# Token gather and expert combination as fp32r products, with the small loads on ScalarE's queue

## The chip, the cores and the metric

The kernel runs on one core of a Trainium2 chip. The metric is the device time of one execution in microseconds (us), median of several runs. In the text TensorE, VectorE, ScalarE, GpSimd and SyncE stand for the rows PE, DVE, ACT, POOL and SP.

## The reference

Two transformer blocks with conditioning, and a second model block behind them, on one sequence of 256 tokens of width 1024. There are three mixers, and behind each stands a mixture of 32 experts, of which every token uses two. Cut to the expert layer:

```python
def _hier_moe(h, w_group, b_group, w_expert, b_expert, w1, w3, w2):
    g_sel = argmax(h @ w_group + b_group)             # one of 4 groups
    top_v, top_i = top_k(expert logits of the group, 2)
    gate = p_g * softmax(top_v)
    ...
    xr = xt[tok]                                      # tokens of expert e
    y = (silu(xr @ w1[e]) * (xr @ w3[e])) @ w2[e]     # 1024 -> 512 -> 1024
    return segment_sum(y * w_row, token)              # weighted sum back to the tokens
```

All data are fp32; the weights of one expert layer are 32 x 3 x 1024 x 512 x 4 bytes, 201 MB.

## The kernel before

The program runs even mixer, expert stage 0, odd mixer, expert stage 1, mixer of the second block, expert stage 2, final norm. Weights stream through a ring of 18 slots in SBUF, 1 MB each (8 KB per partition). `Net.pump` takes a free slot and issues one DMA on SyncE's queue for the next weight piece in a planned order; `done` gives a slot back when the product that read it is emitted, and pumps again; `release` gives back slots held for other things; `reserve` keeps some free slots from the stream for later use. In stage 2 a few further slots ("more") are at hand. So the stream runs ahead by at most the ring, and when the ring is full it stops until a product gives a slot back.

An expert stage (`moe`) has 16 pairs of experts. Before the pairs `route` finds each token's experts and its rank within an expert (`mk` the mask, a triangular product for the ranks, `rk` the rank, `wt` the weight), and `overflow` holds a branch for experts with more than CAP = 64 tokens, which is not taken here. Pair p then does, in TensorE's order:

- `up(p, "g")`, `up(p, "u")`: the two up products, with 4 slots each. `sg` is the silu of the first; `hh` is the product of both.
- `gather(p+1)`: the token matrix `h` (256 tokens x 1024, normalised, in one ring slot) times a one-hot `u` (token to place), fp32, 128 columns; VectorE and ScalarE write the result to `xg` with scale and shift (`affine`).
- `gather_w(p+1)`: transposes the weighted one-hot `uw` to `pg`.
- `turn(p)`: transposes `hh` to `ht`. `down(p)`: the down product with 4 slots, evicted to `y` with the gate factor `ga`.
- `combine(p, t)`: `pg` times `y`, fp32, added by VectorE to token tile t of `x`. For pair p-1 it runs between the products of pair p.

The last pair uses `down_last`, which makes the down product and the addition in four pieces. At pair 0, behind the first up product, `start` emits work for the next stage, and with it small loads: the attention bias (`bias_load`) and router weights (`router`) in stage 0, router weights and constants of the second block (`second_setup`) in stage 1. They are issued on GpSimd's queue, which has nothing else to do there and runs ahead.

A fp32 matmul appears as two records in the trace, an fp32r one as one.

## Time and profile before

| | |
|---|---|
| runs | 2140.69, 2144.75, 2133.42 us; median 2140.69 |
| profiled execution | span 2133.2 us; no time of its own is given beside the span |
| TensorE busy | 2020.9 us, 95% of the span |
| VectorE, ScalarE, GpSimd busy | 793.1, 405.3, 256.1 us |
| DMA | 725.46 MB, 340 GB/s on the mean, 400 to 404 GB/s in most slices of the expert stages |

Busy time is a mean over stages with different limits: the mixers lie near slices 1 to 4, 14 to 17 and 26 to 31 of 40, where the DMA rate is low, and the expert stages between and behind them. The span of the profiled execution stands 7.5 us below the median of the runs and 0.2 below the lowest.

### The profile page before, as it was taken

The numbers are of one execution on the slowest core, as the hardware profiler recorded it, in microseconds if no ns is written. First come the engines' busy times: TensorE is split into PE (matmuls) and PEld (weight loads), VectorE is DVE, ScalarE is ACT, GpSimd is POOL, SyncE is SP. The second block draws the span as 40 slices with busy tenths as digits, with TensorE's granted clock in tenths as the row PEclk, the third lists the DMA queues.
The fourth block names the chain that finished last, engine by engine and source line by source line (L and its number), as shares of the span: only waits on it lengthen the run. The fifth ranks groups of instructions, "written<-read, shape, count | busy, mean of one in ns | idle before, by whom it ended". The sixth has DMA issues, their size and how long they took to land. (4 is left out here: it accounts for less than half of the span.)

```text
span 2133.2 us, 26516 instructions
## 1 busy us (share of the span) xinstructions
PE 2020.9 (95%) x10698; PEld 1077.0 (50%) x10698; DVE 793.1 (37%) x1576; ACT 405.3 (19%) x836; POOL 256.1 (12%) x202
## 2 busy tenths in 40 slices
PE   6889899999999998899999999998899999999997
PEld 3646444434443767543444434686887443444443
DVE  3665222222222667322222222467666122222222
ACT  1423100100000343200000000254543100100101
POOL 1422000000000343200000000143433000000000
PEclk8998999999999999999999999999999999999999
DMA  9797999999999866999999999922457999999997
GB/s 318 245 321 297 366 400 402 403 400 401 404 400 390 311 226 237 336 403 400 400 404 400 400 403 402 310 93 66 133 217 257 381 403 401 400 402 403 400 401 267
DMA packets 279205, 725.46 MB, mean 340 GB/s; under 512 B 18267, under 2 KB 33587, under 8 KB 279069
## 3 DMA queue, kind: packets, MB, share of 16 engines
q1 hardware_dynamic: 269776, 716.84, 88.9%
q0 software_dynamic: 1456, 3.59, 0.6%
q10 hardware_dynamic: 7836, 3.17, 0.6%
q8 instruction: 91, 1.49, 0.3%
q14 instruction: 46, 0.37, 0.0%
HBM read 722.48 MB, written 1.07 MB: 339 GB/s over the span
## 5 line engine op out<-in xcount | busy, mean ns | idle before, releaser
L256 PE MATMUL ps<-slot,xg 128*64 128x512 f32 x2952 | 666.4, 601 | 20.0 <-PEq L1712 12.1
L256 PEld LDWEIGHTS ps<-slot,xg 128*64 128x64 f32 x2952 | 209.3, 138 | 458.6 <-issue 419.6
L256 PE MATMUL ps<-slot 128*128 128x256 f32 (+8 forms) x2230 | 370.4, 327 | 13.9 <-DVE slot L457 9.5
L256 PE MATMUL ps<-slot,ht 128*64 128x512 f32 (+1 forms) x1592 | 343.3, 572 | 6.4 <-DVE ht L249 3.5
L256 PEld LDWEIGHTS ps<-slot 128*128 128x128 f32 (+3 forms) x2230 | 301.4, 187 | 73.2 <-issue 12.9
L1860 DVE TENSOR_TENSOR x<-x,ps 128x512 f32<-128x512 f32 x180 | 120.8, 684 | 322.0 <-PE ps L256 321.2
L256 PEld LDWEIGHTS ps<-slot,ht 128*64 128x64 f32 x1592 | 113.9, 138 | 222.5 <-issue 181.0
L458 POOL TENSOR_TENSOR slot<-slot 128x512 fp32r<-128x512 f32 (+2 forms) x108 | 165.0, 1545 | 263.9 <-ACT slot L456 242.5
L256 PEld LDWEIGHTS ps<-u,slot 128*128 128x128 f32 x1536 | 175.1, 192 | 37.2 <-issue 36.5
L256 PE MATMUL ps<-y,pg 128*128 128x512 f32 (+1 forms) x408 | 187.0, 582 | 0.0
L256 PE MATMUL ps<-u,slot 128*128 128x128 f32 x1536 | 184.2, 278 | 0.0
L1825 DVE TENSOR_TENSOR hh<-sg,ps 128x512 f32<-128x512 f32 x48 | 50.6, 1054 | 340.6 <-PE ps L256 325.6
L1821 ACT ACTIVATE sg<-ps 128x512 f32<-128x512 f32 x48 | 28.7, 597 | 606.4 <-PE ps L256 606.4
L457 DVE TENSOR_TENSOR slot<-slot 128x512 fp32r<-128x512 f32 (+2 forms) x108 | 110.4, 1036 | 53.1 <-ACT slot L456 52.8
L374 POOL TENSOR_TENSOR xr<-xr,mhalf 128x2 f32<-128x2 f32 x7 | 5.0, 711 | 1022.1 <-DVE xr L373 1004.7
L456 ACT CAST slot<-slot 128x1024 fp32r<-128x1024 f32 (+2 forms) x108 | 106.6, 1020 | 46.3 <-PE ps L256 27.3
L256 PEld LDWEIGHTS ps<-y,pg 128*128 128x128 f32 x408 | 69.5, 190 | 86.3 <-issue 84.7
L394 ACT ACTIVATE xg<-ps,cf 128x128 f32<-128x128 f32 x128 | 48.5, 457 | 317.5 <-PE ps L256 317.5
L1850 DVE TENSOR_TENSOR y<-ps,ga 128x512 f32<-128x512 f32 x60 | 41.5, 692 | 171.3 <-PE ps L256 171.3
L398 DVE TENSOR_SCALAR xg<-ps,cf 128x128 f32<-128x128 f32 x128 | 43.9, 404 | 81.0 <-PE ps L256 80.8
L1889 POOL TENSOR_TENSOR slot<-x,rows 128x512 f32<-128x512 f32 x2 | 2.6, 1276 | 480.2 <-DVE x L1885 480.2
L256 PE MATMUL ps<-slot,condz 128*32 128x512 f32 x384 | 48.0, 620 | 6.6 <-DMA slot<-ada_w 6.6
(349 smaller groups left out, 1337.8 us busy)
## 6 DMA issues: line engine op xcount, KB each, us to landing
slot<-moe_w SPq DMA_DIRECT2D x376, 1024.0 KB, 16.8
slot<-w_gate SPq DMA_DIRECT2D x57, 1024.0 KB, 16.2
slot<-w_up SPq DMA_DIRECT2D x56, 1024.0 KB, 20.5
slot<-w_down SPq DMA_DIRECT2D x55, 1024.0 KB, 21.0
slot<-ada_w SPq DMA_DIRECT2D x48, 1024.0 KB, 8.8
slot<-w_in SPq DMA_DIRECT2D x20, 1024.0 KB, 4.8
slot<-odd_w_in SPq DMA_DIRECT2D x12, 1024.0 KB, 13.4
slot<-even_w_in SPq DMA_DIRECT2D x9, 1024.0 KB, 16.9
```

What stands on the lines that cost most here:

```text
L256: self.nc.tensor.matmul(out, lhsT=lhsT, rhs=rhs, start=start, stop=stop)
L374: self.nc.gpsimd.tensor_tensor(out, out, self.mhalf[:, :cols], op=OP.pow)
L394: self.nc.scalar.activation(out, p, AF.Identity, scale=a, bias=nb[:, k:k + 1])
L398: self.nc.vector.tensor_scalar(out, p, a, nb[:, k:k + 1], op0=OP.mult, op1=OP.add)
L456: nc.scalar.copy(wh, src)
L457: nc.vector.tensor_sub(wl[:, 0], src[:, 0], wh[:, 0].bitcast(FT))
L458: nc.gpsimd.tensor_sub(wl[:, 1], src[:, 1], wh[:, 1].bitcast(FT))
L1821: nc.scalar.activation(sg, ps, AF.Silu)
L1825: nc.vector.tensor_mul(hh.rearrange("s k p -> s p k"), st["sg", p].rearrange("s (p k) -> s p k", k=4), ps.rearrange("s (p k) -> s p k", k=4))
L1850: nc.vector.tensor_mul(y[:, sl], ps, self.ga[:, sl])
L1860: nc.vector.tensor_add(self.x[:, t, sl], self.x[:, t, sl], ps)
L1889: (nc.gpsimd, nc.vector)[n % 2].tensor_mul(fo[:, :, sl], xs, fw[:, None, sl].to_broadcast([P, NT, T]))
```

## The change

The gather and the combination become fp32r products. The token matrix is kept as a rounded part `hh` and a remainder `hl`, in two ring slots instead of one; `u` is 0 or 1 for four experts at once, and each gather serves two pairs with 256 columns. The transposed weighted one-hot becomes a 0/1 mask `pg`, and a sum over it, `ws`, one weight for each place, that is multiplied into `hh` of the experts (renamed `ha`). The down product is split into `yh` and `yl` by `parts`, and a combination adds the products of both. All DMAs of GpSimd's queue go to ScalarE's. The mixers end with `reserve=2`, and the slots of the token matrix are released at pair 13.

```diff
     def bias_load(self, i, raw):
         v = self.bvec
-        self.nc.gpsimd.dma_start(raw, bass.AP(tensor=v.tensor, offset=v.offset + i * 8 * 384,
+        self.nc.scalar.dma_start(raw, bass.AP(tensor=v.tensor, offset=v.offset + i * 8 * 384,
...
-        self.release(5, reserve=1)
+        self.release(5, reserve=2)
...
             self.S[nm] = g.tile(shape, FT, name=nm)
-            nc.gpsimd.dma_start(self.S[nm], src)
+            nc.scalar.dma_start(self.S[nm], src)
...
-        nc.gpsimd.dma_start(br[:, 0:4], bg.to_broadcast([P, 4]))
-        nc.gpsimd.dma_start(br[:, 4:36], be.to_broadcast([P, 32]))
...
+        nc.scalar.dma_start(br[:, 0:4], bg.to_broadcast([P, 4]))
+        nc.scalar.dma_start(br[:, 4:36], be.to_broadcast([P, 32]))
...
         nc.vector.tensor_mul(v4(mk), gb, r4(ob))
+        rest()
         p = self.psum((P, NT, E))
...
-            h = self.slot().rearrange("p (t k q) -> p t k q", t=NT, k=KC)
+            hh, hl = (self.slot(FR).rearrange("p (t k q) -> p t k q", t=NT, k=KC) for i in range(2))
             r = self.x_rstd()
             self.route_turn(1)
             self.route_logits(1)
             xv = self.x.rearrange("q t (p k) -> q t k p", k=KC)
-            nc.scalar.activation(h[:, 0], xv[:, 0], AF.Copy, scale=r[:, 0:1])
-            nc.gpsimd.tensor_scalar(h[:, 1], xv[:, 1], r[:, 1:2], None, op0=OP.mult)
-            rk, wt, ti, finish, late = self.route(g, r, mods)
+            for t in range(NT):
+                nc.scalar.activation(hh[:, t], xv[:, t], AF.Copy, scale=r[:, t:t + 1])
+            h0 = g.tile([P, KC, 2 * P], FT, name="xg").rearrange("p (t k) q -> p t (k q)", t=NT)[:, 0]
+            h0 = h0.rearrange("p (k q) -> p k q", k=KC)
+            nc.gpsimd.tensor_scalar(h0, xv[:, 0], r[:, 0:1], None, op0=OP.mult)
+            nc.gpsimd.tensor_sub(hl[:, 0], h0, hh[:, 0].bitcast(FT))
+
+            def rest():
+                nc.vector.scalar_tensor_tensor(hl[:, 1], xv[:, 1], r[:, 1:2], hh[:, 1].bitcast(FT),
+                                               op0=OP.mult, op1=OP.subtract)
+
+            rk, wt, ti, finish, late = self.route(g, r, mods, rest)
             NP = E // 2
             st = {}
             if l == 2:
                 fw = self.rows[1]
-            bc = lambda a, p: a[:, :, 2 * p:2 * p + 2, None].to_broadcast([P, NT, 2, CAP])
-
-            def onehot(p):
-                u = g.tile([P, NT, 2, CAP], FT, name="u", bufs=2)
-                nc.vector.tensor_tensor(u, self.iota[:, None, None, :].to_broadcast([P, NT, 2, CAP]), bc(rk, p),
+            bc = lambda a, e, n: a[:, :, e:e + n, None].to_broadcast([P, NT, n, CAP])
+
+            def onehot(j):
+                u = g.tile([P, NT, 4, CAP], FR, name="u", bufs=2)
+                nc.vector.tensor_tensor(u, self.iota[:, None, None, :].to_broadcast([P, NT, 4, CAP]), bc(rk, 4 * j, 4),
                                         op=OP.is_equal)
-                st["u", p] = u
+                st["u", j] = u
 
             def weighted(p):
-                uw = g.tile([P, NT, 2, CAP], FT, name="uw", bufs=2)
-                nc.vector.tensor_mul(uw, st["u", p], bc(wt, p))
+                uw = g.tile([P, NT, 2, CAP], FT, name="uw")
+                u = st["u", p // 2][:, :, p % 2 * 2:p % 2 * 2 + 2].bitcast(FT)
+                nc.vector.tensor_mul(uw, u, bc(wt, 2 * p, 2))
                 st["uw", p] = uw
 
-            def gather(p):
-                xg = g.tile([P, KC, P], FT, name="xg")
-                m = 4 if p else 2
-                for k0 in range(0, KC, m):
-                    ps = self.psum((P, P * m))
-                    for k in range(m):
+            def gather(j):
+                xg = g.tile([P, KC, 2 * P], FT, name="xg")
+                u = st["u", j].rearrange("p t a s -> p t (a s)")
+                for k0 in range(0, KC, 2):
+                    ps = self.psum().rearrange("p (k s) -> p k s", k=2)
+                    for k in range(2):
                         for t in range(NT):
-                            self.mm(ps[:, P * k:P * k + P], h[:, t, k0 + k], st["u", p][:, t], t == 0, t == NT - 1)
-                    for k in range(m):
-                        self.affine(xg[:, k0 + k], ps[:, P * k:P * k + P], k0 + k, "av"[k0 // m % 2])
-                st["xg", p] = xg
+                            for i, part in enumerate((hh, hl)):
+                                self.mm(ps[:, k], part[:, t, k0 + k], u[:, t], t + i == 0, t + i == 2)
+                    for k in range(2):
+                        self.affine(xg[:, k0 + k], ps[:, k], k0 + k, "av"[k])
+                st["xg"] = xg
 
             def gather_w(p):
                 ps = self.psum((P, T))
                 for t in range(NT):
                     self.tr(ps[:, P * t:P * t + P], st["uw", p][:, t].rearrange("p a s -> p (a s)"))
-                pg = g.tile([P, T], FT, name="pg", bufs=2)
-                self.copy(pg, ps, "a")
-                st["pg", p] = pg
+                pg = g.tile([P, T], FR, name="pg", bufs=2)
+                nc.vector.tensor_scalar(pg, ps, 0.0, None, op0=OP.is_gt)
+                ws = g.tile([P, 1], FT, name="ws", bufs=2)
+                nc.vector.tensor_reduce(ws, ps, axis=AX.X, op=OP.add)
+                st["pg", p], st["ws", p] = pg, ws
...
-                        self.mm(ps[64 * s:64 * s + 64], st["xg", p][:, k, 64 * s:64 * s + 64],
+                        self.mm(ps[64 * s:64 * s + 64], st["xg"][:, k, p % 2 * P + 64 * s:p % 2 * P + 64 * s + 64],
...
-                    hh = g.tile([P, 512], FT, name="hh").rearrange("p (k s) -> p k s", k=4)
-                    nc.vector.tensor_mul(hh.rearrange("s k p -> s p k"),
-                                         st["sg", p].rearrange("s (p k) -> s p k", k=4),
-                                         ps.rearrange("s (p k) -> s p k", k=4))
-                    st["hh", p] = hh
+                    ha = g.tile([P, 512], FT, name="hh").rearrange("p (k s) -> p k s", k=4)
+                    nc.vector.scalar_tensor_tensor(ha.rearrange("s k p -> s p k"),
+                                                   st["sg", p].rearrange("s (p k) -> s p k", k=4), st["ws", p],
+                                                   ps.rearrange("s (p k) -> s p k", k=4), op0=OP.mult, op1=OP.mult)
...
+            def parts(p, sl, ps):
+                if sl.start == 0:
+                    st["y", p] = [g.tile([P, D], FR, name=nm) for nm in ("yh", "yl")]
+                yh, yl = (y[:, sl] for y in st["y", p])
+                if gate:
+                    y = g.tile([P, 512], FT, name="sg", bufs=2)[:, :sl.stop - sl.start]
+                    nc.vector.tensor_mul(y, ps, self.ga[:, sl])
+                    nc.scalar.copy(yh, y)
+                    nc.gpsimd.tensor_sub(yl, y, yh.bitcast(FT))
+                else:
+                    nc.scalar.copy(yh, ps)
+                    nc.vector.tensor_sub(yl, ps, yh.bitcast(FT))
...
             def combine(p, t):
                 for n in range(2):
                     ps = self.psum()
                     sl = slice(512 * n, 512 * n + 512)
-                    self.mm(ps, st["pg", p][:, P * t:P * t + P], st["y", p][:, sl], True, True)
+                    for i, y in enumerate(st["y", p]):
+                        self.mm(ps, st["pg", p][:, P * t:P * t + P], y[:, sl], i == 0, i == 1)
                     nc.vector.tensor_add(self.x[:, t, sl], self.x[:, t, sl], ps)
...
             weighted(0)
             for p in range(NP):
                 last = p == NP - 1
                 if last:
-                    self.reserve += slots
+                    self.reserve += max(0, slots - 2)
                     if l == 2:
                         fo = self.slot().rearrange("p (t d) -> p t d", t=NT)
                 else:
-                    onehot(p + 1)
+                    if p % 2:
+                        onehot(p // 2 + 1)
                     weighted(p + 1)
                 if last:
                     up(p, "g", lambda: combine(p - 1, 0))
                     up(p, "u", lambda: combine(p - 1, 1))
-                    self.release()
                     turn(p)
                 else:
                     up(p, "g")
                             nc.scalar.dma_start(fw, self.A["final_norm_2"].rearrange("(o n) -> o n", o=1)
                                                 .to_broadcast([P, D]))
                     up(p, "u")
-                    gather(p + 1)
+                    if p % 2:
+                        gather(p // 2 + 1)
+                        if p == NP - 3:
+                            self.release(2, reserve=min(2, slots))
```

SyncE issues the weight loads. Here is its order around stage 0's branch (L1711 to L1726; `moe_w` are expert weights), before:

```order
L192 DMA slot<-moe_w 128x2x1024 x8
L192 DMA slot<-moe_w 128x4x512 x4
L192 DMA slot<-moe_w 128x2x1024 x4
L1711 TENSOR_LOAD ti
L1712 COMPARE_AND_BRANCH
```

and after the change:

```order
L193 DMA slot<-moe_w 128x2x1024 x8
L193 DMA slot<-moe_w 128x4x512 x4
L193 DMA slot<-moe_w 128x2x1024 x3
L1713 TENSOR_LOAD ti
L1714 COMPARE_AND_BRANCH
```

One weight load has moved from ahead of the branch to behind it: 15 instead of 16.

VectorE's order in `route` between the mask and the one-hot, before:

```order
L1662 TENSOR_TENSOR mk<-ohg,ob 128x64
L1669 SCALAR_TENSOR_TENSOR rk<-ps,mk 128x64
L1670 TENSOR_SCALAR rk<-rk 128x64
L1779 TENSOR_TENSOR u<-km,rk 128x256
L1678 TENSOR_REDUCE top<-rk 128x1
```

and after the change:

```order
L1663 TENSOR_TENSOR mk<-ohg,ob 128x64
L1779 SCALAR_TENSOR_TENSOR slot<-x,xr,slot 128x1024
L1671 SCALAR_TENSOR_TENSOR rk<-ps,mk 128x64
L1672 TENSOR_SCALAR rk<-rk 128x64
L1791 TENSOR_TENSOR u<-km,rk 128x512
L1680 TENSOR_REDUCE top<-rk 128x1
```

The remainder of token tile 1 (`rest`) has come in between mask and rank, and `u` is twice as wide.

ScalarE's order at the first pair of stage 0, before (`sg` is the silu of the first up product):

```order
L1821 ACTIVATE sg<-ps 128x512
L247 COPY pg<-ps 128x256
L247 COPY ga<-ps 128x512 x2
L394 ACTIVATE xg<-ps,cf 128x128 x4
L247 COPY pg<-ps 128x256
L1821 ACTIVATE sg<-ps 128x512
```

and after the change:

```order
L1837 ACTIVATE sg<-ps 128x512
L579 DMA bias_1470<-bvec 128x8x256
L248 COPY ga<-ps 128x512 x2
L1589 DMA wr<-moe_w_group 128x8x4
L1590 DMA wr<-moe_w_expert 128x8x32
L1591 DMA br<-moe_b_group 128x4
L1592 DMA br<-moe_b_expert 128x32
L1861 CAST yh<-sg 128x512 x2
L1837 ACTIVATE sg<-ps 128x512
```

The bias and router loads stand behind the silu, the copies of `pg` are gone from ScalarE, and the gather's evictions of pair 0 are gone with the gather, which now follows at pair 1.

## Rows read from the trace of the kernel before

**Rows 1.** The page: span, busy time per engine, DMA share and rate in 40 slices.
```profile
span 2133.2 us, 26516 instructions
...
PE 2020.9 (95%) x10698; PEld 1077.0 (50%) x10698; DVE 793.1 (37%) x1576; ACT 405.3 (19%) x836; POOL 256.1 (12%) x202
...
DMA  9797999999999866999999999922457999999997
GB/s 318 245 321 297 366 400 402 403 400 401 404 400 390 311 226 237 336 403 400 400 404 400 400 403 402 310 93 66 133 217 257 381 403 401 400 402 403 400 401 267
```

**Rows 2.** Busy time in five stretches: four stage starts, one middle; columns in the first row.
```profile
core 0: us, PE busy (x) PEld busy (x) DVE busy (x) ACT busy (x) POOL busy (x), PEclk, DMA share, GB/s
226.00:236.00 10.00, 9.60 (x36) 3.51 (x37) 0.00 (x0) 0.84 (x2) 0.00 (x0) 0.83 0.95 298
252.00:256.00 4.00, 4.00 (x22) 1.56 (x19) 0.69 (x1) 0.00 (x0) 0.00 (x0) 1.00 0.67 207
880.00:890.00 10.00, 9.63 (x35) 3.36 (x36) 0.00 (x0) 0.18 (x1) 3.77 (x7) 0.75 0.85 228
1646.00:1656.00 10.00, 7.46 (x48) 4.80 (x48) 5.12 (x24) 2.84 (x7) 0.00 (x0) 1.00 0.33 111
1100.00:1150.00 50.00, 50.00 (x256) 21.94 (x252) 14.08 (x26) 4.36 (x11) 0.00 (x0) 1.00 1.03 403
```

**Rows 3.** The page's DMA issues: the weight slots, KB each, us to landing.
```profile
slot<-moe_w SPq DMA_DIRECT2D x376, 1024.0 KB, 16.8
```

**Rows 4.** Timeline of TensorE, 576 to 612: start, us, tiles, shapes, count.
```profile
578.99 7.04 PE L256 MATMUL ps<-slot,xg 128*64 128x512 f32 x32
...
594.89 3.84 PE L256 MATMUL ps<-u,slot 128*128 128x128 f32 x32
...
599.22 1.88 PE L256 MATMUL ps<-y,pg 128*128 128x512 f32 x4
...
607.95 4.46 PE L256 MATMUL ps<-slot,xg 128*64 128x512 f32 x20
```

**Rows 5.** Timeline of TensorE, 640 to 707, the end of the first expert stage.
```profile
652.47 1.94 PE L256 MATMUL ps<-slot,xg 128*64 128x512 f32 x8 [0.62 <-DMA slot<-moe_w]
...
660.48 7.09 PE L256 MATMUL ps<-slot,ht 128*64 128x512 f32 x32
```

**Rows 6.** Timeline of TensorE, 1170 to 1362, the end of the second.
```profile
1310.14 1.94 PE L256 MATMUL ps<-slot,xg 128*64 128x512 f32 x8 [0.62 <-DMA slot<-moe_w]
```

**Rows 7.** Timeline of TensorE, 1985 to 2134, the end of the third.
```profile
2100.30 1.94 PE L256 MATMUL ps<-more,xg 128*64 128x512 f32 x8 [0.63 <-DMA more<-w_up]
```

**Rows 8.** Timeline of TensorE: fp32r products of other stages, 24 matmuls each.
```profile
1519.67 3.04 PE L256 MATMUL ps<-slot,wx 128*128 128x256 f32 x24
...
195.98 5.74 PE L256 MATMUL ps<-slot 128*128 128x512 f32 x24
```

**Rows 9.** Groups of instructions by line and shape: busy, mean ns, idle before.
```profile
L1378 DVE TENSOR_TENSOR slot<-slot 128x1024 f32<-128x1024 f32 x1 | 1.2, 1225 | 1.1 <-ACT slot L1377 1.1
...
L1768 ACT ACTIVATE slot<-x,xr 128x1024 f32<-128x1024 f32 x3 | 6.6, 2186 | 1.3 <-POOL xr L374 1.3
...
L458 POOL TENSOR_TENSOR slot<-slot 128x256 fp32r<-128x256 f32 x4 | 3.7, 935 | 10.2 <-ACT slot L456 10.2
...
L1875 DVE TENSOR_TENSOR y<-ps,ga 128x256 f32<-128x256 f32 x8 | 3.4, 425 | 11.5 <-PE ps L256 11.5
```

**Rows 10.** Timeline of VectorE, 204 to 262, behind the rank product.
```profile
216.08 0.23 DVE L1669 SCALAR_TENSOR_TENSOR rk<-ps,mk 128x64 f32<-128x64 f32 x1 [1.01 <-PE ps L256]
...
216.57 0.42 DVE L1779 TENSOR_TENSOR u<-km,rk 128x256 f32<-128x256 f32 x1
```

**Rows 11.** DMA queue of GpSimd, 215 to 240, then 878 to 895: packets, MB, share.
```profile
q0 software_dynamic: 416, 1.21, 15.0%
...
q0 software_dynamic: 624, 1.16, 29.8%
```

**Rows 12.** Timeline of GpSimd, 219 to 224: its DMA issues.
```profile
219.71 0.98 POOL L578 DMA_DIRECT2D bias<-bvec  x1 [6.90 <-DVE wt L1697]
```

More of the change, by code (lines that the diff above doesn't have):

```diff
@@ L30 @@
 SLOT = 2048
+SCRATCH = 2048
 EVEN = (1, 1, 4, 1, 1, 2, 2)
@@ L1565, in second @@
             self.weave(self.nsa_prep(g), self.nsa_attn(g, sc), self.hgrn(g, q8), stream())
-        self.release(6, reserve=1)
+        self.release(6, reserve=2)
     def plan_moe(self, l):
@@ L1722, in overflow @@
                     for k in range(4):
-                        self.tr(p[:, k], h[:, t, k0 + k])
+                        for i, part in enumerate(h):
+                            self.mm(p[:, k], part[:, t, k0 + k].bitcast(FT), self.ident, i == 0, i == 1)
                     for k in range(4):
@@ L1728, in overflow @@
                 nc.scalar.dma_start(wc, wd[bass.ds(e, 1)].rearrange("e p t -> (e p) t"))
-                ho = g.tile([P, 4, T], FT, name="y")
+                ho = g.tile([P, 4, T], FT, name="ho", tag="yh")
                 chunk = lambda tag: g.tile([P, 512], FT, name=tag)
@@ L1836, in turn @@
                 st["ht", p] = ht
+            def parts(p, sl, ps):
[10 more added lines that the diff above has]
+                    nc.vector.tensor_sub(yl, ps, yh.bitcast(FT))
             def down(p):
-                y = g.tile([P, D], FT, name="y")
                 for n in range(2):
@@ L1848, in down @@
                     self.done((l, "d", p, 2 * n), (l, "d", p, 2 * n + 1))
-                    if gate:
-                        nc.vector.tensor_mul(y[:, sl], ps, self.ga[:, sl])
-                    else:
-                        self.copy(y[:, sl], ps, "av"[n])
-                st["y", p] = y
+                    parts(p, sl, ps)
             def combine(p, t):
@@ L1873, in piece @@
                     self.done((l, "d", p, n))
-                    if gate:
-                        nc.vector.tensor_mul(y[:, sl], ps, self.ga[:, sl])
-                    else:
-                        self.copy(y[:, sl], ps, "a")
+                    parts(p, sl, ps)
                 def add(n):
@@ L1882, in add @@
                     for t in range(NT):
-                        self.mm(ps[:, t], st["pg", p][:, P * t:P * t + P], y[:, sl], True, True)
+                        for i, y in enumerate(st["y", p]):
+                            self.mm(ps[:, t], st["pg", p][:, P * t:P * t + P], y[:, sl], i == 0, i == 1)
                     xs = self.x[:, :, sl]
```

16 lines of the change are left out of this document (8 added, 8 removed).

## The prediction

> **What bounds the kernel now.** I read the page first. TensorE is busy for most of the span, which would make it the bound, but the slices say otherwise: through most of the three expert stages the DMA row stands at 9 and the rate lies flat near 400 GB/s [rows 1]. The fifth window of [rows 2] puts numbers on it: 50 us in the middle of the second stage, DMA share 1.03, 403 GB/s. One weight slot is 1024 KB [rows 3], that is 1,048,576 B / 403 GB/s = 2.60 us, and a pair of experts has 12 slots, so the stream needs 31.2 us per pair. TensorE's timeline gives its own need: from 578.99 to 607.95 one pair takes 28.96 us [rows 4]. TensorE is therefore the faster of the two; it starts each stage behind a full ring and catches up with the stream. In the first stage it meets it only at pair 14: the wait of 0.62 us before 652.47 ends on a landing [rows 5]; in the second such waits repeat up to 1310.14 [rows 6], in the third up to 2100.30 [rows 7]. After the last of them TensorE works off what is left. The length of a stage is thus the time when its last-waited slot lands plus TensorE's work behind that. I call this landing W.
>
> Where does the stream lose time? Only where the ring is full and nothing is given back: at the start of each stage. The first four windows of [rows 2] give it against 403: 226 to 236 loses 10 x (1 - 298/403) = 2.6 us, 252 to 256 (TensorE gathers and turns, and gives back no slot) 4 x (1 - 207/403) = 1.9, 880 to 890 4.3, 1646 to 1656 7.2. Everything that moves W is decided there.
>
> **TensorE's work in a pair.** The gather of a pair, 32 records, takes 3.84 us, a combination of one token tile 1.88 [rows 4]. An fp32r matmul of 256 columns takes 3.04/24 = 0.127 us and one of 512 columns 5.74/24 = 0.239 [rows 8]. The new gather has 32 matmuls of 256 columns for two pairs: 4.05 us instead of 7.68. The new combination has 4 of 512 columns per tile: 0.96 instead of 1.88. So TensorE saves (7.68 - 4.05)/2 + 2 x 0.92 = 3.7 us per pair at most; in odd pairs eight evictions of 256 columns stand on VectorE ahead of the copy to ht, at 0.425 us or more each [rows 9], 3.4 us where TensorE has 1.0 of combination to do; averaged over both pairs that gives about 1.2 to 1.4 back, and TensorE's pair is near 26.7 us. Over 48 pairs that is more than 100 us, and I count none of it: the stream needs 31.2, TensorE will only wait more. It counts behind W alone.
>
> **Gains behind W.** In the first stage W is 652.47 and the second half of pair 14's down product starts at about 660.48 + 3.5 = 664.0, W + 11.5 [rows 5]. Its last slot lands four slots behind W, at W + 10.4, so of the shorter gather only about 1.0 counts. Then two combinations, 0.92 each: 1.9. In the last pair four add products halve (about 0.5 each, 2.0), but the eviction before each becomes three steps: VectorE 0.425 and a ScalarE cast, then a GpSimd subtraction, where 256 columns took 0.935 [rows 9]; about 1.5 of the 2.0 is given back. Together 3.4 us, and as much in the second stage. In the third the last waits lie inside the last pair [rows 7], and only 0.4 (one combination, against the next landing) and 1.4 of the tail remain: 1.8. Gains: 8.6 us.
>
> **Losses before W.** (a) *A slot less.* The token matrix now takes two ring slots. SP's order shows 15 weight loads ahead of the branch where there were 16, in all three stages one less. The ring is full at the start, so each stage loads one slot later: 3 x 2.6 = 7.8. The bounds are 0 (if the ring had not filled) and 7.8; the idle windows of [rows 2] put it at the upper end. The Trainium skill (DMA: Bandwidth & Descriptors, section Specifications) gives about 358 GB/s as a core's share of HBM. By it a slot would take 2.93 us and this term be 8.8. The trace moves 403 and the sum goes by that.
>
> (b) *The first product starts later.* VectorE now computes a 128x1024 remainder between mk and rk, and the one-hot u doubles (0.42 to about 0.8). A plain 128x1024 VectorE operation on contiguous data takes 1225 ns; a ScalarE pass over the same strided reading takes 2186 [rows 9]. So 1.2 to 2.4 us, of which 1.01 lies in the wait for the rank product that stands there anyway [rows 10]. With u: 0.6 to 1.8 later; I take 1.2, as a single-input stride is what slowed the ScalarE pass, and here one of two inputs is strided. Gather, first product and first give-back all follow: 3 x 1.2 = 3.6.
>
> (c) *The small loads.* Before, GpSimd's queue moved the bias and the router weights of the first stage while the ring was full, 1.21 MB at 15.0% of 25 us = 3.75 us of all engines; in the second stage 1.16 MB, 29.8% of 17 us = 5.07 [rows 11]. They ran in those idle windows, free. Now ScalarE issues them behind its first silu, when slots are coming back and the weight stream has work: each us that they take moves W. By bytes at 403 they need 3.0 and 2.9; by the queue's records 3.75 and 5.07. I take 3.7 (1 MB in one large piece, so what was recorded) and 3.6 (small pieces can overlap with others'). Sum 7.3, bounds 5.9 and 8.8, or 0 if they still find idle time.
>
> (d) *Shared lanes.* ScalarE's DMAs wait, like SP's, for the DMA eight places earlier in the common sequence; GpSimd's had lanes of their own. In the second stage 15 loads stand between weight loads. I take 1.0 (0 to 6).
>
> (e) *One stall goes.* Pair 0 no longer gathers, so the give-back pause at 252 to 256 shrinks from 6 us to under 3: -2.0 (0 to -2.0).
>
> (f) The first mixer's ScalarE issues five DMAs that GpSimd issued: 0.5. The longest GpSimd issue took 0.98 us [rows 12], so 0 to 4.9.
>
> VectorE and ScalarE work that is added inside the pairs (mask, sum of weights, cast, remainder) lies beside 12 weight slots per pair; VectorE was 37% busy [rows 1]. If that cover went, the ht copy would be the first to be late, and it delays TensorE, not the stream.
>
> **Sum.** 7.8 + 3.6 + 7.3 + 1.0 - 2.0 + 0.5 = 18.2 lost, 8.6 gained: +9.6 us on the profiled span of 2133.2. That span equals the lowest of the three runs and lies 7.5 below their median of 2140.69; their mean is 2139.6. Against the mean: 2149.
>
> **Rivals.** *The stream gets faster (ends faster than before).* If the weight stream's pace depends on how soon TensorE gives slots back, a quicker TensorE speeds it up. 576 slots at 2.565 us instead of 2.60 save 20 us: 2129; from 408 GB/s on it decides. Against it: the share of 1.03 in [rows 2] leaves the engines no free time, and the rate is as flat where TensorE waits as where it lags [rows 1]. The Trainium skill (DMA: Bandwidth & Descriptors, section Latency and other measured facts) guesses that GpSimd's descriptor rings slow two of the DMA engines; without its DMAs the stream might then gain. No row here shows such an effect: the flat stretches ran without that queue. Chance 0.12.
>
> *The start costs are hidden.* If the small loads land before the stream has work and the ring's lost slot is refilled within the same idle spell, (a) to (d) vanish, and -8.6 - 2.0 stays: about 2130. For it: the third stage idles 7.2 us [rows 2], more than a slot. Against it: idle time there is the ring being full, which a smaller ring lengthens. Chance 0.15.
>
> *Shared lanes block SP (slower).* A weight load queued behind a ScalarE load that itself waits idles the stream; with (c), (b) at the upper ends (+1.5, +1.8) and (d) at 6: +18 or more, 2158 to 2165. It decides once SP pauses over 2 us after the first give-back. Chance 0.18.
>
> **How the numbers follow.** The forecast, 2142 to 2157, has 0.55. 0.5% is 10.7 us, about what a measurement can tell from no change; so faster is under 2130.0, slower over 2151.4. The forecast gives 0.38 same and 0.17 slower; the faster stream 0.12 faster; hidden costs 0.06 faster and 0.09 same; lanes 0.18 slower. Together 0.18, 0.47, 0.35. The range 2128 to 2162 leaves out about half of the first and third rival's weight.
>
> **What would show it.** Right: in the first 20 us of each stage the rate falls lower or longer than in [rows 2]; TensorE's gather for two pairs near 4 us, its waits on weight slots starting by pair 5 or so and about 4.5 us per pair; 403 GB/s in the middle; W later by 4 to 8 us in the first two stages, and the work behind W shorter by 3. Wrong: a middle rate above 406, TensorE without waits on slots, or W no later than before. A pair in which TensorE still needs over 31 us would show that evictions, not the stream, set the pace.

## The result and the profile after

The changed kernel takes 2153.55 us (median of 8 runs, 2146.87 to 2158.83), the kernel before 2138.47 (median of 8 runs); the ratio is 1.0065, 95% interval 1.0046 to 1.0084. It is slower by 0.65%, over the bound of 0.5% by less than the interval is wide.

The page of the changed kernel, in the rows that answer to [rows 1]:

```profile
span 2147.6 us, 24992 instructions
...
PE 1905.7 (89%) x9930; PEld 1016.1 (47%) x9930; DVE 833.0 (39%) x1574; ACT 427.2 (20%) x778; POOL 331.0 (15%) x248
...
DMA  9697899999999966899999999921366899999998
GB/s 318 234 319 284 325 401 404 400 400 403 401 400 396 329 234 235 306 391 400 402 403 400 401 404 401 317 99 55 123 220 250 340 403 400 401 404 400 400 402 304
```

TensorE is busy 115 us less than before, and the span is 14.4 us longer. The flat 400 GB/s of the three expert stages has not moved; the slices at each stage's start have become lower (284 and 325 where 297 and 366 stood, 306 for 336, 340 for 381).

The busy time in six stretches, to be read against [rows 2] (us, engines, PEclk, DMA share, GB/s). The three stage starts are taken as far behind the stage's first router product as there:

```profile
core 0: us, PE busy (x) PEld busy (x) DVE busy (x) ACT busy (x) POOL busy (x), PEclk, DMA share, GB/s
229.00:239.00 10.00, 7.36 (x34) 2.85 (x34) 2.37 (x5) 2.08 (x3) 0.00 (x0) 1.00 0.62 201
...
258.00:268.00 10.00, 10.00 (x46) 3.46 (x44) 2.89 (x5) 1.22 (x2) 2.13 (x2) 1.00 1.01 385
...
884.20:894.20 10.00, 7.32 (x35) 2.80 (x34) 2.55 (x5) 1.89 (x3) 0.00 (x0) 1.00 0.62 201
...
902.00:918.00 16.00, 14.33 (x70) 4.93 (x68) 4.76 (x8) 1.24 (x2) 2.73 (x2) 1.00 0.90 267
1658.00:1668.00 10.00, 8.19 (x40) 6.50 (x41) 6.58 (x24) 1.68 (x5) 0.00 (x0) 0.66 0.02 8
1100.00:1150.00 50.00, 44.09 (x212) 18.56 (x208) 14.92 (x25) 5.33 (x9) 5.26 (x4) 1.00 1.04 400
```

The middle is as it was (400 GB/s at a share of 1.04), but TensorE fills 44.09 of those 50 us instead of 50.00. The starts have fallen from 298 to 201 GB/s, from 228 to 201 and from 111 to 8: at the third the stream stands still for nearly ten microseconds. From 902 to 918, where ScalarE's small loads of stage 1 run, the DMA engines move 267 GB/s in all.

The landing that decides each stage's end (the last slot of pair 14's u product in the first two stages, the second slot of pair 15's in the third), in TensorE's timeline; [rows 5 to 7] are the same of before. In the third stage of the changed kernel one short wait of 0.21 us follows, for the fourth slot:

```profile
662.14 1.94 PE L257 MATMUL ps<-slot,xg 128*64 128x512 f32 x8 [0.62 <-DMA slot<-moe_w]
...
1321.68 1.94 PE L257 MATMUL ps<-slot,xg 128*64 128x512 f32 x8 [0.62 <-DMA slot<-moe_w]
...
2118.73 1.94 PE L257 MATMUL ps<-slot,xg 128*64 128x512 f32 x8 [0.52 <-DMA slot<-w_up]
```

What such a row is worth shows when it is read against the first router product of its own stage, so that earlier stages drop out. This table is worked out in that way from TensorE's timeline of each profiled execution (us from the stage's first router product, stages 0 / 1 / 2):

| kernel | runs' median | first up product | that slot's landing |
|---|---|---|---|
| before | 2138.47 | 21.2 / 21.0 / 18.3 | 447.2 / 450.8 / 465.2 |
| changed | 2153.55 | 23.4 / 23.5 / 23.2 | 453.9 / 458.1 / 471.6 |
| a_pool | 2150.83 | 26.0 / 23.7 / 22.5 | 455.5 / 452.3 / 470.6 |
| a_early | 2162.55 | 28.2 / 31.9 / 23.2 | 457.6 / 461.4 / 471.6 |
| a_stt | 2160.65 | 23.5 / 23.7 / 23.4 | 456.4 / 460.6 / 472.1 |
| a_ring19 | 2145.80 | 24.3 / 23.5 / 23.3 | 452.5 / 454.8 / 469.5 |
| a_sp | 2155.88 | 23.4 / 23.8 / 23.1 | 456.4 / 459.9 / 471.9 |
| a_spe19 | 2140.28 | 25.0 / 24.0 / 23.2 | 448.8 / 453.0 / 468.9 |
| a_nolo | 2149.07 | 21.3 / 21.2 / 21.0 | 454.6 / 457.3 / 469.8 |
| b_slot | 2137.36 | 21.3 / 20.9 / 20.4 | 447.9 / 451.0 / 469.4 |
| b_hold | 2141.82 | 21.4 / 20.9 / 18.2 | 450.0 / 450.7 / 468.2 |

The changed kernel's landings come 6.7, 7.3 and 6.4 us later: 20.4 us. Names with a_ start from the changed kernel, with b_ and c_ from the one before.

Pair by pair, TensorE in stage 0 (the gather for two pairs, the down products of pairs 2 and 3, the first wait on a slot):

```profile
274.20 4.01 PE L257 MATMUL ps<-u,slot 128*128 128x256 f32 x32
...
307.68 7.09 PE L257 MATMUL ps<-slot,ht 128*64 128x512 f32 x32 [1.49 <-issue]
...
336.79 7.09 PE L257 MATMUL ps<-slot,ht 128*64 128x512 f32 x32 [1.49 <-issue]
...
431.34 1.94 PE L257 MATMUL ps<-slot,xg 128*64 128x512 f32 x8 [0.45 <-DMA slot<-moe_w]
```

The gather for two pairs takes 4.01 us. The down product of one pair starts 29.1 us behind that of the pair before, that of the next 26.4 (from 281.29 to 307.68): 27.75 on the mean, where the stream needs 31.2. The first wait on a slot in this stage comes at 431.34, in pair 7; before it came in pair 14.

### The profile page after: what moved, and what is told of

Its sections match the earlier page's. It is cut to its first block, busy times and chain, and to the rows that moved or that the text cites. A ratio compares the mean times of both kernels' runs of the same rounds, so it can differ in the third digit from the quotient of the medians.

```text
span 2147.6 us, 24992 instructions
## 1 busy us (share of the span) xinstructions
PE 1905.7 (89%) x9930; PEld 1016.1 (47%) x9930; DVE 833.0 (39%) x1574; ACT 427.2 (20%) x778; POOL 331.0 (15%) x248
## 5 line engine op out<-in xcount | busy, mean ns | idle before, releaser
L257 PE MATMUL ps<-slot,xg 128*64 128x512 f32 x2992 | 699.0, 601 | 55.8 <-DMA slot<-moe_w 33.3
L257 PEld LDWEIGHTS ps<-slot 128*128 128x128 f32 (+3 forms) x2230 | 300.0, 186 | 74.0 <-issue 15.1
L1862 POOL TENSOR_TENSOR yl<-sg,yh 128x512 fp32r<-128x512 f32 (+1 forms) x68 | 84.5, 1243 | 910.0 <-ACT yh L1861 910.0
L1841 DVE SCALAR_TENSOR_TENSOR hh<-sg,ws,ps 128x512 f32<-128x512 f32 x48 | 53.5, 1114 | 343.9 <-PE ps L257 188.2
L1861 ACT CAST yh<-sg 128x512 fp32r<-128x512 f32 (+1 forms) x68 | 40.3, 593 | 491.5 <-DVE sg L1860 477.9
L1860 DVE TENSOR_TENSOR sg<-ps,ga 128x512 f32<-128x512 f32 (+1 forms) x68 | 44.9, 660 | 186.2 <-PE ps L257 186.2
L257 PEld LDWEIGHTS ps<-u,slot 128*128 128x128 f32 x768 | 95.5, 196 | 18.3 <-issue 17.0
L257 PE MATMUL ps<-u,slot 128*128 128x256 f32 x768 | 100.4, 290 | 0.0
L257 PE MATMUL ps<-yh,pg 128*128 128x512 f32 (+1 forms) x204 | 86.9, 428 | 0.7 <-ACT yh L1861 0.7
L257 PE MATMUL ps<-yl,pg 128*128 128x512 f32 (+1 forms) x204 | 77.5, 383 | 0.9 <-POOL yl L1862 0.8
L395 ACT ACTIVATE xg<-ps,cf 128x256 f32<-128x256 f32 x64 | 36.1, 564 | 160.4 <-PE ps L257 160.4
```

The lines of the kernel that those rows point to most:

```text
L257: self.nc.tensor.matmul(out, lhsT=lhsT, rhs=rhs, start=start, stop=stop)
L395: self.nc.scalar.activation(out, p, AF.Identity, scale=a, bias=nb[:, k:k + 1])
L1841: nc.vector.scalar_tensor_tensor(ha.rearrange("s k p -> s p k"), st["sg", p].rearrange("s (p k) -> s p k", k=4), st["ws", p], ps.rearrange ...
L1860: nc.vector.tensor_mul(y, ps, self.ga[:, sl])
L1861: nc.scalar.copy(yh, y)
L1862: nc.gpsimd.tensor_sub(yl, y, yh.bitcast(FT))
```

## The experiments

**When the small loads run, and from which queue.** a_pool gives the small loads back to GpSimd:

```diff
-        self.nc.scalar.dma_start(raw, bass.AP(...))      # and the router's and second_setup's
+        self.nc.gpsimd.dma_start(raw, bass.AP(...))
```

> The changed kernel with the small loads of the stages (bias, router, constants) issued by GpSimd again, at their old place in the program. Theory (the losses arise at the stage starts, each once): the loads run again in the window where the ring is full; stage 0, from its first router product to the first product of the next stage, falls from 504.2 to about 501 us, stage 1 from 511.3 to about 504, stage 2 stays at 500.4; in all 8 to 11 us less than the changed kernel, about 2143. Rival 1 (the loads cost only their bytes wherever they run, and the loss of stage 1 comes from later releases): stages 0 and 1 change by under 1 us. Rival 2 (the new evictions slow every pair): no stage changes.

Measured: 2150.83 us, ratio to before 1.0059 (1.0039 to 1.0079), which can't be told from the changed kernel. The landings say more. In stage 1 it comes 5.8 us earlier, as expected; in stage 0 it comes 1.6 later. There GpSimd issues the bias load ahead of the branch, and TensorE waits longer at it:

```profile
234.67 10.02 PE L257 MATMUL ps<-slot,xg 128*64 128x512 f32 x32 [5.13 <-PEq L1714]
```

After 5.13 us of waiting the product of four slots takes 10.02 us, at a granted clock of 0.70 (the mean of a stretch; 1.00 is the upper of TensorE's two levels, 2.4 GHz, 0.50 the lower, 1.2); in the changed kernel it waits 2.68 us and takes 7.09, at 1.00. Before the change it was as here, 4.98 and 8.73, at 0.81:

```profile
226.40 8.73 PE L256 MATMUL ps<-slot,xg 128*64 128x512 f32 x32 [4.98 <-PEq L1712]
```

a_early leaves them on ScalarE, but ahead of the branch:

```diff
+            if early is not None:
+                early()          # bias_load, router, second_setup, out of start()
             if late is not None:
                 late()
```

> The changed kernel with the same loads still issued by ScalarE, but ahead of the branch, when the ring is full. Theory (it is the time at which the loads run that costs, not the queue): stage 0 near 501 us, stage 1 near 504 to 505, the whole about 2143 to 2145, as with GpSimd. Rival (ScalarE's queue and its shared lanes are the cost): stage 1 stays near 511 us, or the first silu comes later by the 7 us that 15 issues take, and stage 0 stays near 504.

Measured: 2162.55 us, ratio 1.0104 (1.0062 to 1.0145). My theory fell here, nearly as the rival had it. TensorE now waits for ScalarE's queue at the branch:

```profile
236.59 8.88 PE L257 MATMUL ps<-slot,xg 128*64 128x512 f32 x32 [7.41 <-ACTq L1714]
...
900.88 4.53 PE L257 MATMUL ps<-slot,xg 128*64 128x512 f32 x10 [10.40 <-ACTq L1714]
```

7.41 and 10.40 us, and the first up products start 28.2 and 31.9 us behind the router product.

a_sp puts the loads on SyncE's queue, at the changed kernel's place:

```diff
-            nc.scalar.dma_start(self.S[nm], src)         # and five more
+            nc.sync.dma_start(self.S[nm], src)
```

> The changed kernel with the small loads on SyncE's queue, at the same place in the program, between weight loads, none on ScalarE. It tells the queue from the bytes. Theory, with the lanes that two queues share as the second part of the loads' cost: on one queue no load waits on the other's lane; the DMA share no longer falls under 0.95 in the 20 us in which the loads run (0.79 and 0.83 in stage 1 of the changed kernel), and stage 1 falls by 1.5 to 3 us, stage 0 by 0 to 1; about 2150. Rival (small pieces are slow by themselves): the share falls as before and nothing changes.

Measured: 2155.88 us, 1.0087 (1.0064 to 1.011), where about 2150 was expected; no gain. SyncE no longer waits for another queue's DMA in this stretch, but its own issues of small pieces last:

```profile
902.83 5.55 SPq L1590 DMA_DIRECT2D wr<-w_rtr  x1
908.43 3.53 SPq L1591 DMA_DIRECT2D br<-b_grp  x1
```

Two of the 15 take 5.55 and 3.53 us (the second column), the others about half a microsecond, and the weight loads stand behind them:

```profile
910.00:915.00 5.00, 3.54 (x18) 1.20 (x14) 2.19 (x4) 0.00 (x0) 0.00 (x0) 1.00 0.45 90
915.00:920.00 5.00, 4.78 (x24) 1.64 (x26) 0.85 (x2) 0.26 (x1) 0.00 (x0) 1.00 0.67 164
```

The DMA share falls to 0.45 and 0.67. So neither queue makes the loads cheap at this place. How long an issue lasts is not fixed by the load: in the changed kernel's stage 1 the load that takes 5.55 us here took 0.79 on ScalarE's queue, and the one behind it 4.02.

a_spe19 puts them on SyncE ahead of the branch, behind the loads that fill the ring, and has 19 slots. Its pair is a_ring19, the changed kernel with 19 slots and nothing else:

```diff
-RING = 18
+RING = 19
-SCRATCH = 2048
+SCRATCH = 512
...
-                u = g.tile([P, NT, 4, CAP], FR, name="u", bufs=2)
+                u = g.tile([P, NT, 4, CAP], FR, name="u", bufs=1)
```

> The changed kernel with 19 ring slots instead of 18 (room from a smaller scratch and one u buffer), so that each stage has as many weight slots loaded ahead of its branch as before the change. Theory (a ring slot is worth 2.6 us per stage, because the ring is full at each start): each expert stage about 2.6 us shorter, 501.6, 508.7 and 497.8, the mixers the same within 1 us, 8 us in all, about 2146. Rival (the slot is refilled within the idle time anyway): under 2 us in all.

> The changed kernel with 19 slots and the small loads on SyncE's queue ahead of the branch, behind the weight loads that fill the ring. Theory (their cost is the time at which they run; ScalarE, which had to reach the branch, was what made the earlier place slow): the branch is not later than in the changed kernel (23.4 us behind the first router product), the loads run while the ring is full, stage 0 is 3 us and stage 1 5 to 7 us shorter than with 19 slots alone; about 2136 to 2138. Rival (SyncE comes late to the branch and to the first slot that is given back): the first slots are issued over 3 us late, no gain against 19 slots alone, about 2146.

Measured: a_ring19 2145.80 us, 1.0036 (1.0024 to 1.0048), 7.75 us under the changed kernel where 8 was expected; the landings move by 1.4, 3.3 and 2.1, together 6.8. a_spe19 2140.28 us, 1.0011 (1.0001 to 1.0022): another 5.5 us. It was expected at 2136 to 2138: the landing in stage 0 comes 3.7 us earlier than a_ring19's, but in stage 1 only 1.8. So a slot and the place of the small loads bring back 13.3 of the 15.1 us between the medians. That doesn't make them the whole loss, since the medians also hold what the change gains behind the landings: a_spe19's landings still come 1.6, 2.2 and 3.7 us later than the kernel before's, 7.5 of the 20.4, and what is left over there fits the later start of the stages, which no run took out alone without a new loss.

**The slot, from the other side.** b_slot takes the kernel before and lets each stage hold one slot more:

```diff
             h = self.slot().rearrange("p (t k q) -> p t k q", t=NT, k=KC)
+            idle = self.slot()
+            nc.gpsimd.memset(idle[:, :8], 0.0)
...
-        self.release(5, reserve=1)
+        self.release(5, reserve=2)
```

> The kernel before with nothing changed but the ring: each expert stage holds one further slot that it does not use, with the changed kernel's reserve and release, so that 15, 15 and 17 weight loads stand ahead of the branch. Theory (a slot is worth the time of one load at each stage start): the expert stages get 2.6 us longer each, 505.5 to 508.1, 507.9 to 510.5 and 498.1 to 500.7, the mixers stay, in all 8 us, about 2146. Rival (the slot is refilled within the idle time): under 2 us in all, about 2139.

Measured: 2137.36 us, 0.9995 (0.9984 to 1.0006). It missed, because the edit didn't hold the slot: nothing read it later, and the first weight load behind the branch took it. (Its stages are counted up to a product 4.6 us further on than in the expectation of a_pool.) What it shows is that one load moved behind the branch costs nothing on the whole, and nearly nothing in the first two landings (0.7 and 0.2). In the third stage it did cost: there the load flew while TensorE waited at the branch, the wait grew from 2.28 to 4.33 us, the first product took 10.08 us at a granted clock of 0.70, and the landing came 4.2 us later:

```profile
1653.72 10.08 PE L256 MATMUL ps<-slot,xg 128*64 128x512 f32 x32 [4.33 <-PEq L1712]
```

b_hold has a reader at pair 13:

```diff
+                    if p == NP - 3:
+                        nc.vector.tensor_copy(idle[:, 8:16], idle[:, :8])
+                        self.release(1, reserve=min(1, slots))
```

> As b_slot, but the further slot is really kept: in b_slot the first weight load behind the branch took it at once, since nothing read it later; here VectorE copies 8 columns of it at pair 13. Theory (a ring slot is worth the time of a load at each start): the last waited landing comes 2.6 us later behind the first router product in each stage (449.8, 453.4, 467.8), in all about 8 us, 2146. Rival (with GpSimd's loads in the idle window the slot costs less): the landings move by under 1 us in stages 0 and 1 and only stage 2 gets longer, about 2141.

Measured: 2141.82 us, 1.0018 (1.0009 to 1.0028): between theory and rival. The landings come 2.8 us later, 0.1 earlier and 3.0 later. A slot costs the time of a load in stages 0 and 2, and nothing in stage 1. Why stage 1 differs stays open: GpSimd's loads, the rival's reason, run at the start of stage 0 too.

**The remainder of the token matrix.** In the changed kernel's routing (VectorE, then GpSimd):

```profile
214.80 0.23 DVE L1652 TENSOR_TENSOR em<-lg,ohg 128x64 f32<-128x64 f32 x1
...
216.19 2.06 DVE L1646 TENSOR_TENSOR oh<-km,i 128x16 f32<-128x16 f32 x1
...
219.88 2.06 DVE L1779 SCALAR_TENSOR_TENSOR slot<-x,xr,slot 128x1024 fp32r<-128x1024 f32 x1
...
221.87 0.21 DVE L1671 SCALAR_TENSOR_TENSOR rk<-ps,mk 128x64 f32<-128x64 f32 x1
```

```profile
211.91 3.86 POOL L1775 TENSOR_SCALAR xg<-x,xr 128x1024 f32<-128x1024 f32 x1
215.86 2.36 POOL L1776 TENSOR_TENSOR slot<-xg,slot 128x1024 fp32r<-128x1024 f32 x1
```

A product of 128x16 took 2.06 us, up to the end of GpSimd's subtraction; ahead of it, during GpSimd's scaling from 211.91, one of 128x64 took 0.23. a_stt computes both remainders on VectorE:

```diff
             def rest():
-                nc.vector.scalar_tensor_tensor(hl[:, 1], xv[:, 1], r[:, 1:2], ...)
+                for t in range(NT):
+                    nc.vector.scalar_tensor_tensor(hl[:, t], xv[:, t], r[:, t:t + 1], ...)
```

> The changed kernel with both remainders of the token matrix on VectorE, none on GpSimd. In the changed kernel a 128x16 product on VectorE in the routing took 2.06 us instead of 0.17, while GpSimd subtracted on 128x1024. Theory (VectorE waited for GpSimd's subtraction): that product takes 0.17 again, a second 2.06 us remainder follows the first, and the rank is ready about 0.2 us later than in the changed kernel; the whole the same within 2 us. Rival (the 2.06 us have another cause): the product stays at 2.06 and the rank comes 2 us later; every stage start moves by 2 us, the whole 6 us longer, about 2160.

```profile
215.56 0.17 DVE L1646 TENSOR_TENSOR oh<-km,i 128x16 f32<-128x16 f32 x1
...
217.36 4.01 DVE L1776 SCALAR_TENSOR_TENSOR slot<-x,xr,slot 128x1024 fp32r<-128x1024 f32 x2
...
221.31 0.20 DVE L1671 SCALAR_TENSOR_TENSOR rk<-ps,mk 128x64 f32<-128x64 f32 x1
```

The 128x16 product takes 0.17 us again and the remainders 2.0 each; the first up product starts as late as in the changed kernel. So the wait was for GpSimd's subtraction. The Trainium skill (SBUF — State Buffer, section SBUF: two separate sides) says that a VectorE instruction with two SBUF inputs and a GpSimd instruction that reads SBUF lock a shared pair of ports, and that whichever starts first keeps it for its whole length. The trace agrees for GpSimd's subtraction, which has two inputs. For the scaling, which reads SBUF too but with one input, it does not: from 211.91 to 215.77 five two-input VectorE instructions ran at 0.17 to 0.23 us.

The whole, however, is 2160.65 us (1.0103, 1.008 to 1.0127), 7 us above the changed kernel where 2 were expected. The landings are 2.5 us later in stages 0 and 1, though the starts are equal. SyncE's waits in stage 1 point to the place:

```profile
SPq L193 <- DMA br<-b_grp: 10.8, 1, 10.8
SPq L193 <- DMA k_vmask<-k_vmask: 8.3, 1, 8.3
```

Weight loads waited 10.8 and 8.3 us for two of ScalarE's small loads. In the changed kernel they waited, in the same stage:

```profile
SPq L193 <- DMA slot<-moe_w: 8.7, 2, 6.6
...
SPq L193 <- DMA k_ropec<-k_ropec: 7.2, 1, 7.2
```

Their total is nearly the same (17.6 with a last one of 1.7, against 19.1 in a_stt); what differs is how they fall. SyncE's issues of weight loads while ScalarE's small loads ran, in the changed kernel and then in a_stt:

```profile
901.17 8.34 SPq L193 DMA_DIRECT2D slot<-moe_w  x2
```

```profile
911.24 0.56 SPq L193 DMA_DIRECT2D slot<-moe_w  x1
```

In the changed kernel two weight loads were issued in the 15 us between 894.5 and 909.7, in a_stt one in the 20 us between 900.4 and 920.2. The DMA engines moved 283 GB/s from 40 to 50 us behind the router product in the one and 199 in the other; in stage 0 it was 350 and 229. Why the two queues fell into step so differently stays open.

a_nolo leaves the remainder out (zeros in its place):

```diff
+            for t in range(NT):
+                nc.gpsimd.tensor_scalar(hl[:, t].rearrange("p k q -> p (k q)"), self.x[:, t], 0.0, None, op0=OP.mult)
             def rest():
-                nc.vector.scalar_tensor_tensor(hl[:, 1], ...)
+                pass
```

> The changed kernel with zeros in the place of the remainder of the token matrix (left out: the low part of the token matrix; GpSimd writes zeros from contiguous data, VectorE nothing). Ring, gather and loads as in the changed kernel. Theory (the remainder delays the stage start, 1.9 us by VectorE's wait for GpSimd and 0.9 by the rest ahead of the rank): the rank is ready 2.8 us earlier, the first up product starts 20.6 us behind the first router product instead of 23.4, the landings come 2.5 us earlier in each stage and more in stage 2, in all 8 us, about 2145. Rival (the branch waits for something else, as SyncE's or TensorE's own sequencer): the first up product starts less than 1 us earlier, about 2152.

Measured: 2149.07 us, 1.005 (1.0035 to 1.0065), which overlaps the changed kernel's interval. The starts are 2.1 to 2.3 us earlier, but the landings 0.7 later, 0.8 and 1.8 earlier: only in stage 2, where a single small load runs, does the start carry over. In stages 0 and 1 part of it is lost at the start itself: TensorE waits 3.8 us at the branch instead of 2.7, and its first product takes 8.78 us at a granted clock of 0.80, so that it ends only 0.4 and 0.6 us earlier. In stage 0:

```profile
232.37 8.78 PE L257 MATMUL ps<-slot,xg 128*64 128x512 f32 x32 [3.82 <-PEq L1714]
```

The rest goes where the small loads run: from 40 to 50 us behind the router product the DMA engines moved 303 instead of 350 GB/s in stage 0, 218 instead of 283 in stage 1.

**The combination alone, and the fastest kernel.** c_comb is the kernel before with the new combination, as in the change's diff (`gather_w`, `ha`, `parts`, `combine`, `down_last`). b_ring19 is the kernel before with 19 slots; c_comb19 is both. All three have the smaller scratch that the changed kernel has too.

```diff
-RING = 18
+RING = 19
...
-    nc = bacc.Bacc("TRN2", target_bir_lowering=False, num_devices=1)
+    nc = bacc.Bacc("TRN2", target_bir_lowering=False, num_devices=1, dynamic_dma_scratch_size=2048)
```

> The kernel before with the new combination alone (mask, weight in the gated product, split y, two fp32r products); gather, ring and loads as before. Theory (TensorE's saving counts only behind the last wait on a slot): TensorE's pair falls by 1.8 us, the landing of the last waited slot stays within 1 us of 447.2, 450.8 and 465.2 us behind the first router product, and each stage gets 1.5 to 2.5 us shorter behind it; about 2133. Rival 1 (TensorE's pairs set the pace of stage 0 until pair 14): stage 0 gets over 10 us shorter. Rival 2 (three-step evictions cost more than the products save): the stages get longer.

> The kernel before with 19 ring slots (room from a smaller scratch for GpSimd's DMAs), nothing else. Theory: one more load ahead at each start, the landings 2.6 us earlier in stage 2, which idles longest, and 1 to 2.6 in stages 0 and 1; 5 to 8 us in all, 2131 to 2134, the fastest kernel so far. Rival (ring not the bound before the change): under 2 us.

> As b_ring19 with the new combination as well. Theory, as c_comb left it (TensorE's saving inside the pairs turns into waits, and what is saved behind the last landing is lost to TensorE's clock in the last pair): within 2 us of b_ring19. Rival (c_comb hid a gain of 5 us behind a chance): 5 us faster than b_ring19.

Measured: c_comb 2137.64 us, 0.9999 (0.9987 to 1.0011). The expected 5 us did not come. In stage 0 the work behind the landing is 2.4 us shorter, as expected, but the landing itself comes 2.2 us later (449.4), which the expectation had kept within 1 us; why stays open. By 590 TensorE waits on slots there (the first row). Stage 1 is 2.6 us longer, and its last pair runs slower (the second row); stage 2 is 1.3 shorter:

```profile
593.43 1.94 PE L256 MATMUL ps<-slot,xg 128*64 128x512 f32 x8 [0.63 <-DMA slot<-moe_w]
...
1353.46 5.36 PE L256 MATMUL ps<-slot,ht 128*64 128x256 f32 x32 [0.79 <-DVE ht L249]
```

32 matmuls that take 3.67 us at the same place of the kernel before take 5.36. b_ring19: 2128.39 us, 0.9955 (0.9938 to 0.9971), faster than both kernels, with stages 2.4, 0.7 and 2.6 us shorter than before; in its stage 0 TensorE no longer waits on a slot at all; c_comb19: 2130.05, 0.9961 (0.9946 to 0.9976), the same as b_ring19.

## Why the prediction was right

2149 was forecast, in 2128 to 2162; 2153.55 came, inside the forecast's own range of 2142 to 2157. Of the three outcomes the one with 0.35 came, slower over 0.5%, by a margin of 0.15%.

The sum came out near: the landings are 20.4 us later, where the losses ahead of them were summed to 17.7; the work behind them is 6.8 us shorter, where 8.6 was summed; the mixers add 0.7. That makes up 14.3 of the 14.4 us between the spans of the two profiled executions. Part of it is luck, since the terms were wrong in both directions. Taken back one after the other, the slot gave 6.8 us on the landings (7.8 in the sum), the loads' place another 6.1 (8.3), and 7.5 were left for the later start and the pause (1.6).

*The stream bounds the stages, TensorE's saving is hidden:* right. 115 us less TensorE work changed no middle rate, and TensorE waits. Its pair takes 27.75 us against the 26.7 that I gave it; in each pair it stands idle for 0.8 to 1.5 us ahead of the transposes of `hh` or of the down product. The prediction's reason for such waits was misread: it put eight evictions of 256 columns on VectorE in every second pair, but `affine` puts four there and four on ScalarE. What stands ahead of the copy to `ht` in every pair is the mask `pg` and the sum `ws`, 0.42 and 0.41 us (at 306.23 and 306.57).

*(a) A slot less, 7.8:* right on the changed kernel (with the slot given back 7.75 by the medians, 6.8 by the landings; that edit also cut the scratch and one `u` buffer). In the kernel before it is 5.7 by the landings.

*(b) Later start, 3.6:* mis-sized. The starts came 2.2, 2.5 and 4.9 us later, 9.6 together. Missing was VectorE's wait for GpSimd's subtraction, 1.9 in each stage: the gather starts 3.2 to 3.4 us later than before in all three stages. Missing too was what came back at the branch in stages 0 and 1, where GpSimd's loads no longer ran: the wait fell from 4.98 and 4.88 to 2.68 us, and the first product from 8.73 and 9.41 to 7.09, so that it ended only 0.6 and 0.2 us later than before. In the third stage nothing could be given back, since the wait at the branch was short before (the last row, of the kernel before), and TensorE's clock fell:

```profile
220.11 0.83 PE L257 MATMUL ps<-mk,km 128*128 128x32 f32 x6 [2.30 <-DVE mk L1663]
...
223.82 5.14 PE L257 MATMUL ps<-u,slot 128*128 128x256 f32 x32
...
231.64 7.09 PE L257 MATMUL ps<-slot,xg 128*64 128x512 f32 x32 [2.68 <-DVEq L1714]
...
1658.85 0.86 PE L257 MATMUL ps<-mk,km 128*128 128x32 f32 x6 [2.58 <-DVE mk L1663]
...
1662.56 5.92 PE L257 MATMUL ps<-u,slot 128*128 128x256 f32 x32
...
1670.33 7.09 PE L257 MATMUL ps<-slot,xg 128*64 128x512 f32 x32 [1.85 <-PEq L1714]
```

```profile
1653.47 2.80 PE L256 MATMUL ps<-slot,xg 128*64 128x512 f32 x12 [2.28 <-PEq L1712]
```

In the third stage the changed kernel's gather took 5.92 us behind waits of 2.58 and 0.96, in a stretch with a granted clock of 0.66 (0.50, the lower level, from 1660 to 1664, behind these waits); in stage 0 it took 5.14. On the landings the start counted in full only in stage 2.

*(c) and (d), loads and lanes, 8.3:* the sum was somewhat too large, and its parts were not right. By the records the loads took 4.7 and 5.3 us of the engines. Beside that SyncE waited up to 5.9 us (stage 0) and 7.2 us (stage 1) at a time on ScalarE's loads, which I had at 1.0 and as a rival: by the rival's own sign, a pause of over 2 us, it is what happened, only not at its price. a_stt, with the same loads at the same place, loses 5 us more on the landings. That these waits are the cost was not shown: a_sp has none of them and lands later still, in stage 1 behind issues of 5.55 and 3.53 us. The Trainium skill (DMA: Bandwidth & Descriptors, section Issuing engines are not separate DMA queues) says that another issuing engine saves only issue time. The runs agree that behind the first product neither SyncE's nor ScalarE's queue made the loads cheap; the issue time itself was not small, since a few took 3.5 to 6.6 us each and held up what stood behind them.

*(e) The pause at pair 0, -2.0:* right; from 258 to 268 the changed kernel has 385 GB/s.

*Gains behind W, 8.6:* 6.8 came. In stage 0 it was 3.4, as summed (53.7 us from the landing to the next stage's first product before, 50.3 after), and in stage 2 4.0 where 1.8 was summed (32.9 to the end before, 28.9 after). In stage 1, where 3.4 was summed, there was a loss of 0.6. Products of the changed kernel's last two pairs there, and the same before:

```profile
1327.95 8.20 PE L257 MATMUL ps<-slot,ht 128*64 128x512 f32 x32 [1.49 <-issue]
...
1362.12 5.36 PE L257 MATMUL ps<-slot,ht 128*64 128x256 f32 x32 [0.78 <-DVE ht L250]
```

```profile
1318.15 7.09 PE L256 MATMUL ps<-slot,ht 128*64 128x512 f32 x32
...
1351.36 3.67 PE L256 MATMUL ps<-slot,ht 128*64 128x256 f32 x32 [0.78 <-DVE ht L249]
```

They took 8.20 and 5.36 us instead of 7.09 and 3.67, and the first half of an up product between them 6.59 (at 1339.98) instead of 5.20 (at 1329.08), 4.2 together; the granted clock from 1322 to 1375 was 0.90, before 0.97 from 1310 to 1362. It is tempting to say that a TensorE that waits more runs slower behind its waits. In the third stage the same product goes the other way, before and after:

```profile
2110.37 5.36 PE L256 MATMUL ps<-slot,ht 128*64 128x256 f32 x32 [0.78 <-DVE ht L249]
```

```profile
2128.50 3.67 PE L257 MATMUL ps<-slot,ht 128*64 128x256 f32 x32 [0.78 <-DVE ht L250]
```

There it gave 1.7 of the 4.0 us. In the eight kernels with the changed kernel's ending, the stretch behind the landing takes 50.0 to 52.9 us in stage 0 and 48.5 to 53.3 in stage 1, so that a few us of the clock come and go with the execution; what sets them was not shown.

The first mixer was 3.0 us longer and the second 2.1 shorter in the profiled execution; other kernels with the same mixers have 206.1 to 211.1 us for the first, so I can't tell this from the spread of executions.

## What to carry to other kernels

Where a weight stream bounds a stage, look at its first 20 us: there the ring is full, and a slot taken, a later first product or a load moved out of that window can cost its full time once per stage (here between nothing and all of it), while work saved in the middle was worth nothing. Small loads belong in the window in which the stream stands still, on a queue that has nothing else to reach; what they do to a branch in that window has to be measured with them. Before making products cheaper, try whether the freed memory buys one more slot: here that alone was worth 0.45%.

## What the runs showed of the hardware

- A two-input product of VectorE stood still for 1.9 us while GpSimd subtracted 128x1024; five others ran in 0.17 to 0.23 us each while GpSimd scaled the same amount.
- A load of 128 KB in small pieces held the issuing queue for 5.55 us (SyncE, a_sp) or 6.59 us (ScalarE, stage 0 of the changed kernel), against 0.36 us for one of 256 KB. In stage 1 of the changed kernel a load of the same shape took 0.79 us, and the 2 KB load behind it 4.02.
- TensorE's wait at the branch that is not taken was 1.85 to 2.68 us with the DMA engines nearly idle (under 10 GB/s, three stages of the changed kernel) and 4.88 to 5.13 with GpSimd's loads in flight. It was longer with weight loads in flight alone, too: 4.33 us at 215 GB/s (b_slot, third stage), 3.8 at 111 and 143 (a_nolo). Behind these longer waits the first product took 8.73 to 10.08 us, at a granted clock of 0.70 to 0.81, instead of 7.09 at 1.00. Why the wait is longer stays open.
